# An encoder layer on one core: a block of the second product moved past a product, a half-width root, later stores and waits, eight additions moved to GpSimd

## The chip, the core and the metric

The kernel runs on one core of one Trainium2 chip. The metric is device time of one execution in microseconds (us). A core has five engines that run their own queues in order: TensorE (PE in the profile, with its weight loads as PEld), VectorE (DVE), ScalarE (ACT), GpSimd (POOL) and SyncE (SP), which here only starts DMAs. Data lies in SBUF (128 partitions), matrix products land in PSUM, large arrays in DRAM.

## The reference, cut to what matters

One layer of a transformer encoder for two requests, 512 and 1024 tokens, model width 1024, all in float32. The parts that the change touches are the MLP and the gated embedding behind it:

```
m = _rmsnorm(h, norm_mlp_g)
h = h + jnp.square(jax.nn.relu(m @ w_up)) @ w_down            # 1024 -> 4096 -> 1024
gate = jax.nn.sigmoid(_rmsnorm(h, norm_ple_g) @ w_ple_gate)   # 1024 -> 1024
h = h + gate * (p_i @ w_ple_proj)                             # 256 -> 1024
return _rmsnorm(h, final_norm_g)
```

Ahead of it stand a normalisation, an input projection, attention with rotary positions beside a pooling mixer, and an output projection.

## The kernel before, in words

**Precision.** Every float32 operand is split into a high part in a reduced format and a low part, the rest (a cast on ScalarE, then a subtraction on GpSimd or VectorE). A product is three matmuls: high by high, high by low, low by high (`three`, line 103).

**Tiling.** The 1536 tokens are three chunks of 512, numbered 0 (the short request), 1 and 2. Activations lie transposed, features on partitions. SBUF is 49 equal buffers (`slot`, line 74); a tile takes a free one, and a program orders who waits for whose release.

**The MLP.** Matrix products are done by a scheme with seven products of halves in place of eight (numbered 1 to 7, taken in the order 1, 6, 2, 5, 7, 3, 4), whose sums and differences are made on VectorE. `Pair(c, g)` (line 987) is the up product for 256 of the 4096 hidden features; there are 16 pairs for chunk 0 (`c` = 0) and 16 for chunks 1 and 2 together (`c` = 1, called wide here).
- For chunk 0, `Pair.run` (line 1082) makes the seven products with 256 columns a matmul, in PSUM tiles `px` (products 1 and 2), `py` (6), `pz` (5 and 3) and `pq` (7 and 4), takes Relu and Square, and splits the result into `r` (lines 1119, 1125 high; 1129 low, on VectorE). The down product of a pair is made while the next pair's products run: `between(i)` (line 1629) calls the pair before's `down(i)` for one of four blocks of 12 matmuls of 512 columns each (PSUM tile `pd`), which VectorE adds to `h` (line 1080). In the kernel before, block 0 stands between products 1 and 6, block 1 between 2 and 5, block 2 between 7 and 3, block 3 behind 4.
- For the wide pairs, `Pair.run_wide` (line 1132) makes seven products of 12 matmuls of 512 columns. ScalarE copies product 1 (line 1137) before product 2 may be added to the same PSUM tile. The results are four quarters, `c1` and `c2` with two halves each; `c2`'s second half is ready after product 7, its first half after product 4. Relu and Square of `c2` run over both halves behind product 4 (lines 1162, 1163). `inputs` (line 1166) splits quarters and differences into tiles `ta` (cast in 1172, low part in 1174, differences in 1177) and stores them to DRAM as `T_d`. The down product of the wide pairs comes afterwards (`Double`, line 1181): it loads `T_d` as `tb`, splits weights `v` (casts in 1206), makes blocks `pd`, and evacuates them (1241, 1243) into `H` and `U`, a term shared by parts 2 and 3 of chunk 1's rows and by all four parts of chunk 2's (a part is 256 features).

**Side work.** TensorE's order is written out by hand. After each product, `after(i)` (line 1637) issues one step of what feeds later products: `feed` splits the up weights (cast in line 1009, low part on GpSimd in line 1010, sums on VectorE), `split_down` the down weights, `inputs` and `weights` those above, and then calls `step` (line 603). A step first carries out whatever `later(n, ...)` put off by `n` steps (a first-in-first-out list), then moves each generator in `besides` on by one yield, then the first one in `chores`. So a `wait(n)` in a generator is a wait of `n` steps.

**Loads and stores.** `sy.dma_start` starts a DMA from SP's queue where the scheduler sees fit. `load` (line 55) does the same, and ties the DMA behind the last TensorE instruction written so far.

**The gate.** After the down product, `gate` (line 1699) makes eight output blocks of 128 features for chunk 0, eight for chunk 1, then eight for each half (256 tokens) of chunk 2: 6 matmuls for the projection (`pj`), 24 for the gate (`pg`), then a chain VectorE (1733), ScalarE (1734), VectorE (1735, 1736), ScalarE (1737), and GpSimd, which sums squares (1743). Steps are called behind `pj` and at the places that `HOOKS` (line 1694) names: nine a block for chunk 0, nine for chunk 1 (one in its last block), two a block for chunk 2's first half, three for its second. `gate_in` (1508) makes the next chunk's gate input `hg` (1518 on ScalarE, 1520 on VectorE) in the last block. `split_pp` (1502) splits the embedding in block 6 (1505, 1506).
- `stat(c)` (line 874) finishes chunk `c`'s rows: `lower` adds `U` (line 881) and scales (882) on VectorE, `total` squares on ScalarE and sums on GpSimd (891); 25 steps later `spread_g` makes the reciprocal root and spreads it over the partitions by matmuls (`ssg`, `bcg`). Chunk 1's runs during chunk 0's gate, chunk 2's during chunk 1's.
- `finish(c, o, w, sq)` (line 1745) runs in `chores` behind each group: it waits some steps, sums the squares by matmuls (`ssf`), makes the root, spreads it (`dgf` in line 655, `bcf`), scales (1769) and stores the result.

**The start.** Nine matmuls on a constant tile (`warm`) run before the first data arrives.

Of the kernel before, what the change touches and what calls it, by code (L numbers as in the profile page):

```python
# [12 lines left out]
ALU = mybir.AluOpType  # L13
# [22 lines left out]
def encoder_layer(ctx, tc, xT, xn, xr, pT, w1, w2, w_pool, w_out, w_up, w_down, w_gate, w_proj,  # L36
# [141 lines left out]
    wz = slot([P, CH], mybir.dt.bfloat16, "warm")  # L178
    gp.memset(wz, 1.0)
    wps = tp_ps("warm")  # L180
    for i in range(9):
        pe.matmul(wps, wz[:, 0:P], wz, start=True, stop=True)
    ones_sb = const.tile([P, P], F32R, name="ones_sb")
    gp.memset(as32(ones_sb), 1.0)
# [410 lines left out]
    def later(n, act, *a):  # L595
        aged.append((age[0] + n, act, a))
# [277 lines left out]
    def stat(c):  # L874
        acc = slot([P, 2, CH], F32, f"sqg{c}")

        def lower(a):
            for e in range(2):
                t = hT[c][a][:, e]
                if c == 2 or a > 1:  # L880
                    ve.tensor_tensor(t, t, U[a % 2][:, e], op=ALU.add)
                ve.tensor_tensor(t, t, ws[c], op=ALU.mult)
                yield

        def total(a):
            sq = slot([P, 2, CH], F32, f"sqg{c}{a}") if a else acc
            sc.activation(sq, hT[c][a], AF.Square)
            yield
            for e in range(2):
                if a:  # L890
                    gp.tensor_tensor(acc[:, e], acc[:, e], sq[:, e], op=ALU.add)
                    yield

        yield from staged(range(4), lower, total)
        gp.tensor_tensor(acc[:, 0], acc[:, 0], acc[:, 1], op=ALU.add)
        yield from wait(25)
        yield from spread_g(c, acc)

    def spread_g(c, acc):
        bc = yield from rsqrt_rows([acc[:, 0]], CH, f"g{c}")  # L900
        t = slot([P, CH], F32, f"bcs{c}")
        sc.copy(t, bc)
        if c:
            bcs[c] = t
            yield
            return

        def keep():
            sy.dma_start(bc_d, t)
            made.add("bc")  # L910
        later(2, keep)

    MO, ws, made = {}, {}, set()
    HF = CH // 2
# [72 lines left out]
    class Pair:  # L987
# [94 lines left out]
        def run(self, between, after):  # L1082
# [12 lines left out]
            self.product(1, x)  # L1095
            sc.copy(t, x)
            after(1)
            between(0)
            y = bank("u", "py")
            self.product(6, y)  # L1100
            ve.tensor_tensor(u2, y, t, op=ALU.add)
            after(6)
            self.product(2, x, False)
            sc.activation(c1[:, A], x, AF.Relu)
            after(2)
# [26 lines left out]
        def run_wide(self, after):  # L1132

            c1, c2 = self.X = [slot([P, 2, CH], F32, f"c{self.id}{i}") for i in range(2)]
            x = tp_ps(f"px{self.id}")
            self.product(1, x)
            sc.copy(c1[:, 1], x)  # L1137
            after(1)
            y = ps("u", f"py{self.id}")
            self.product(6, y)  # L1140
            ve.tensor_tensor(c2[:, 0], y, c1[:, 1], op=ALU.add)
            after(6)
            self.product(2, x, False)
            sc.activation(c1[:, 0], x, AF.Relu)
            sc.activation(c1[:, 0], c1[:, 0], AF.Square)
            after(2)
            z = tp_ps(f"pz{self.id}")
            self.product(5, z)
            ve.tensor_tensor(c2[:, 1], z, c2[:, 0], op=ALU.add)
            after(5)  # L1150
            q = ps("u", f"pq{self.id}")
            self.product(7, q)
            ve.tensor_tensor(c2[:, 1], q, c2[:, 1], op=ALU.add)
            after(7)
            self.product(3, z, False)
            ve.tensor_tensor(c1[:, 1], z, c2[:, 0], op=ALU.add)
            sc.activation(c1[:, 1], c1[:, 1], AF.Relu)
            sc.activation(c1[:, 1], c1[:, 1], AF.Square)
            after(3)
            self.product(4, q, False)  # L1160
            ve.tensor_tensor(c2[:, 0], q, c2[:, 0], op=ALU.add)
            sc.activation(c2, c2, AF.Relu)
            sc.activation(c2, c2, AF.Square)
            after(4)

        def inputs(self):
# [3 lines left out]
            for i, x in ((1, b11), (5, b11), (2, b21), (3, b22), (7, b12), (6, b11), (4, b21)):  # L1170
                t = slot([P, 2, CH], F32R, f"ta{self.id}_{i}")
                sc.copy(t[:, 0], x)  # L1172
                yield
                ve.tensor_tensor(t[:, 1], x, as32(t[:, 0]), op=ALU.subtract)  # L1174
                if i in diffs:
                    out, y, z = diffs[i]
                    ve.tensor_tensor(out, y, z, op=ALU.subtract)  # L1177
                later(3, load, T_d[self.g, i], flat(t))
                yield

    class Double:
# [387 lines left out]
    def gating(c):  # L1569
# [14 lines left out]

        def keep(a):
            for i in range(2):
                sy.dma_start(hg_d[a][i], flat(gin[c, a][i]))
            return iter(())

        while "bc" not in made:  # L1590
# [154 lines left out]
    def finish(c, o, w, sq):  # L1745
        tok = slice(o, o + w)
        if not o:
            yield from wait((14, 4, 3)[c])
        bc = yield from rsqrt_rows(sq, w, f"f{c}{o}")
        if o:  # L1750
            bc, b2 = bc
# [34 lines left out]

    while not fed:
        step()
    groups = ((0, 0, CH), (1, 0, CH), (2, 0, CH // 2), (2, CH // 2, CH // 2))
    for c, o, w in groups:  # L1790
        sq = []
# [2 lines left out]
        for d in range(KD):  # L1794
            if c == 0 and d % 2 == 0 and d:
                load_h(0, d // 2, hl_d[d // 2])
            if d == 4 and c < 2:
                load_pp(c + 1)
            if c < 2 and d == KD - 2:
# [86 lines left out]
```

## Time and profile before

| what | value |
|---|---|
| median of 3 runs | 1734.44 us (1734.39 to 1734.63) |
| the profiled execution | 1735.07 us |
| its span, first to last instruction | 1733.3 us |
| matmuls in the trace | 9028 |
| mean granted TensorE clock | 0.998 |
| ScalarE, GpSimd, VectorE busy | 869.1, 1052.5, 1279.5 us |

The profile is one execution, read by the hardware. A row of the order of time gives the start in us from the span's first instruction, the duration, the engine, the line, the operation, output and inputs, and in brackets how long the engine was idle ahead of it and who ended that. Several instructions of a kind are drawn together, with their count. The ends of matmuls are modelled, so that the last one of a row seems to reach into the next row; what one takes is read from start to start. A line can be that of a helper: line 49 is every matmul, line 56 every `load`.

### The profile page before, as it was taken

To read this page: it belongs to the slowest core of one execution; us is meant where nothing else is said; L and a number is where in the kernel's file an instruction comes from. 1 tells how busy PE (TensorE), PEld (TensorE's weight loads), DVE (VectorE), ACT (ScalarE), POOL (GpSimd) and SP (SyncE) were. 2 spreads that over 40 slices of the span, in tenths; PEclk is the share of its full clock that TensorE was granted. 3 is DMA by queue.
4 is the path that set the end of the run, shared out by engine and by line. 5 is a ranking of instruction groups with operands and counts; after the bars stand their busy time and mean duration, and the time that the engine had idled before them with its cause. 6 is when DMAs were issued, how large, how long until landed. Compare 5 with 4: busy or idle time off the path is not lost.

```text
span 1733.3 us, 25333 instructions
## 1 busy us (share of the span) xinstructions
PE 1704.3 (98%) x9028; PEld 1437.7 (83%) x9028; DVE 1279.5 (74%) x1683; ACT 869.1 (50%) x1515; POOL 1052.5 (61%) x844
## 2 busy tenths in 40 slices
PE   9999999999999999999999999999999999999998
PEld 7888878888889988888887787877787877887788
DVE  6676765788887568767757999998676677665865
ACT  6444355667884575565544666666522113224243
POOL 2485983434666678878855455555678765645432
PEclk9999999999999999999999999999999999999999
DMA  7364645120429525643596766667999595941102
GB/s 259 134 217 162 253 176 201 37 98 14 147 110 355 197 91 165 207 143 132 175 380 246 251 251 233 231 242 265 384 393 368 230 349 213 401 168 61 56 18 86
DMA packets 111150, 351.01 MB, mean 203 GB/s; under 512 B 12465, under 2 KB 18993, under 8 KB 111025
## 3 DMA queue, kind: packets, MB, share of 16 engines
q1 hardware_dynamic: 110464, 349.01, 55.0%
q8 instruction: 71, 1.16, 0.3%
q14 instruction: 55, 0.44, 0.1%
q10 hardware_dynamic: 560, 0.40, 0.1%
HBM read 227.20 MB, written 122.16 MB: 202 GB/s over the span
## 4 chain that ended last, share of the span: by engine, by line
PE 38%; DVE 7%; ACT 3%; issue 1%; POOL 1%; DMA 0%; POOLq 0%; ACTq 0%; DVEq 0%
PE pd L49 18%; PE px L49 5%; PE pz L49 4%; PE pq L49 4%; PE pg L49 3%; PE py L49 2%; PE pj L49 1%; DVE ta L1174 1%; DVE hg L1520 1%; DVE s L1735 1%; DVE H L1736 1%; ACT s L1734 1%; DVE c L1177 1%; DVE h L1769 0%; ACT ta L1172 0%
## 5 line engine op out<-in xcount | busy, mean ns | idle before, releaser
L49 PE MATMUL pd<-tb,v 128*128 128x512 f32 x1344 | 315.5, 396 | 3.8 <-ACT Hu L1241 2.0
L49 PEld LDWEIGHTS pd<-tb,v 128*128 128x128 f32 x1344 | 253.2, 189 | 65.4 <-ACT Hu L1241 2.4
L1010 POOL TENSOR_TENSOR w<-ws,w 128x512 fp32r<-128x512 f32 x128 | 185.0, 1450 | 155.5 <-ACT w L1009 155.5
L49 PE MATMUL pd<-r,wd 128*128 128x512 f32 x768 | 191.3, 396 | 6.2 <-DVE r L1129 5.8
L1010 POOL TENSOR_TENSOR w<-wur,w 128x512 fp32r<-128x512 f32 x96 | 154.3, 1620 | 65.9 <-ACT w L1009 62.0
L49 PE MATMUL z<-w,x 128*128 128x512 f32 (+1 forms) x864 | 174.9, 360 | 0.6 <-DVE x L124 0.6
L536 POOL TENSOR_SCALAR pr<-pr,rr 128x1024 f32<-128x1024 f32 (+1 forms) x96 | 94.8, 988 | 126.6 <-DVE rr L534 61.1
L49 PEld LDWEIGHTS pd<-r,wd 128*128 128x128 f32 x768 | 139.5, 188 | 38.1 <-DVE r L1129 9.4
L49 PEld LDWEIGHTS z<-w,x 128*128 128x128 f32 x864 | 144.2, 190 | 26.7 <-issue 1.5
L1212 POOL TENSOR_TENSOR v<-we,v 128x512 fp32r<-128x512 f32 x80 | 117.9, 1498 | 69.8 <-ACT v L1206 49.7
L1174 DVE TENSOR_TENSOR ta<-c,ta 128x512 fp32r<-128x512 f32 x112 | 126.6, 1130 | 30.8 <-ACT ta L1172 30.7
L49 PE MATMUL pg<-hg,wg 128*128 128x512 f32 (+1 forms) x768 | 142.3, 339 | 1.0 <-DVE hg L1520 1.0
L1243 DVE TENSOR_TENSOR H<-pd,H 128x1024 f32<-128x1024 f32 x72 | 87.8, 1222 | 71.1 <-PE pd L49 71.1
L546 ACT CAST pt<-tp 128x512 fp32r<-128x512 f32 x160 | 88.0, 590 | 101.3 <-PE tp L53 100.4
L547 DVE TENSOR_TENSOR pt<-tp,pt 128x512 fp32r<-128x512 f32 x160 | 104.1, 684 | 41.0 <-ACT pt L546 40.8
L49 PEld LDWEIGHTS pg<-hg,wg 128*128 128x128 f32 x768 | 119.2, 188 | 18.1 <-DVE hg L1520 1.6
L1206 ACT CAST v<-we 128x1024 fp32r<-128x1024 f32 x40 | 41.5, 1049 | 164.5 <-DMA we<-in_w_down_dram 73.5
L1172 ACT CAST ta<-c 128x512 fp32r<-128x512 f32 x112 | 69.3, 620 | 107.8 <-DVE c L1177 107.0
L520 DVE TENSOR_REDUCE nm<-S 128x1 f32<-128x1024 f32 (+1 forms) x96 | 100.2, 1044 | 26.6 <-PE S L49 26.1
L530 ACT ACTIVATE pr<-S,nm 128x1024 f32<-128x1024 f32 (+1 forms) x96 | 94.2, 981 | 12.4 <-DMA qs_d<-qs 6.3
L49 PE MATMUL px<-mw,w 128*128 128x512 f32 x384 | 95.3, 397 | 1.6 <-ACT c L1137 1.4
L49 PE MATMUL o<-pt,vs 128*128 128x512 f32 x320 | 93.2, 403 | 0.8 <-DVE pt L547 0.8
(279 smaller groups left out, 3738.0 us busy)
## 6 DMA issues: line engine op xcount, KB each, us to landing
T_d<-ta SPq DMA_DIRECT2D x112, 512.0 KB, 3.0
tb<-T_d SPq DMA_DIRECT2D x112, 512.0 KB, 9.2
wur<-in_w_up_dram SPq DMA_DIRECT2D x64, 512.0 KB, 5.2
wdr<-in_w_down_dram SPq DMA_DIRECT2D x32, 512.0 KB, 4.4
we<-in_w_down_dram SPq DMA_DIRECT2D x32, 512.0 KB, 8.8
mw_d<-mm SPq DMA_DIRECT2D x28, 512.0 KB, 6.2
mw<-mw_d SPq DMA_DIRECT2D x28, 512.0 KB, 10.1
h_d<-h SPq DMA_DIRECT2D x16, 512.0 KB, 3.0
```

The costliest lines, as they stand in the source:

```text
L49: last_pe[0] = nc.tensor.matmul(*a, **k).ins
L520: ve.tensor_reduce(nm, S[:, :nch * CH], axis=AX.X, op=ALU.max, negate=True)
L530: sc.activation(self.pr[j], S[:, :n], AF.Exp, bias=nm, accum_out=self.sums[:, j:j + 1])
L536: gp.tensor_scalar(p, p, rr, 1.0, op0=ALU.mult, op1=ALU.mult)
L546: sc.copy(self.pt[kt][:, 0], tp)
L547: ve.tensor_tensor(self.pt[kt][:, 1], tp, as32(self.pt[kt][:, 0]), op=ALU.subtract)
L1010: gp.tensor_tensor(t[:, 1], x, as32(t[:, 0]), op=ALU.subtract)
L1172: sc.copy(t[:, 0], x)
L1174: ve.tensor_tensor(t[:, 1], x, as32(t[:, 0]), op=ALU.subtract)
L1206: sc.copy(hi, src)
L1212: gp.tensor_tensor(lo[:, p], src[:, p], as32(hi[:, p]), op=ALU.subtract)
L1243: ve.tensor_tensor(H[at], pd, H[at], op=ALU.add)
```

## The change

Nine edits:
1. Ten `warm` matmuls in place of nine.
2. In `stat`, chunk 2's rows are no longer added to `U` on VectorE (chunk 1's still are, for the two of four parts that need it there).
3. A new generator `complete(2)` makes these eight additions on GpSimd, one every `EVERY` = 2 steps, put into `besides` at block `FROM` = 5 of chunk 0's gate, parts in the order 0, 2, 1, 3.
4. In `Pair.run`, `between(0)` moves from behind `after(1)` to behind `after(6)`: block 0 of the pair before's down product comes after product 6.
5. In `run_wide`, Relu and Square of `c2` are split: its second half behind product 7, its first half behind product 4.
6. `T_d` stores are put off by 4 steps in place of 3.
7. The store of the spread root `bc_d` is put off by 4 in place of 2 steps, and is a `load`.
8. The stores of `hg_d` are put off by 4 steps and are `load`s.
9. `finish` waits 14, 6, 4 steps for chunks 0, 1, 2 in place of 14, 4, 3.

```diff
-    for i in range(9):
+    for i in range(10):
         pe.matmul(wps, wz[:, 0:P], wz, start=True, stop=True)
...
         def lower(a):
             for e in range(2):
                 t = hT[c][a][:, e]
-                if c == 2 or a > 1:
+                if c == 1 and a > 1:
                     ve.tensor_tensor(t, t, U[a % 2][:, e], op=ALU.add)
                 ve.tensor_tensor(t, t, ws[c], op=ALU.mult)
                 yield
...
+    def complete(c):
+        for a in (0, 2, 1, 3):
+            for e in range(2):
+                t = hT[c][a][:, e]
+                gp.tensor_tensor(t, t, U[a % 2][:, e], op=ALU.add)
+                yield from wait(EVERY)
...
         def keep():
-            sy.dma_start(bc_d, t)
+            load(bc_d, t)
             made.add("bc")
-        later(2, keep)
+        later(4, keep)
...
             self.product(1, x)
             sc.copy(t, x)
             after(1)
-            between(0)
             y = bank("u", "py")
             self.product(6, y)
             ve.tensor_tensor(u2, y, t, op=ALU.add)
             after(6)
+            between(0)
             self.product(2, x, False)
...
             self.product(7, q)
             ve.tensor_tensor(c2[:, 1], q, c2[:, 1], op=ALU.add)
+            sc.activation(c2[:, 1], c2[:, 1], AF.Relu)
+            sc.activation(c2[:, 1], c2[:, 1], AF.Square)
             after(7)
...
             self.product(4, q, False)
             ve.tensor_tensor(c2[:, 0], q, c2[:, 0], op=ALU.add)
-            sc.activation(c2, c2, AF.Relu)
-            sc.activation(c2, c2, AF.Square)
+            sc.activation(c2[:, 0], c2[:, 0], AF.Relu)
+            sc.activation(c2[:, 0], c2[:, 0], AF.Square)
             after(4)
...
-                later(3, load, T_d[self.g, i], flat(t))
+                later(4, load, T_d[self.g, i], flat(t))
...
         def keep(a):
             for i in range(2):
-                sy.dma_start(hg_d[a][i], flat(gin[c, a][i]))
+                later(4, load, hg_d[a][i], flat(gin[c, a][i]))
             return iter(())
...
         if not o:
-            yield from wait((14, 4, 3)[c])
+            yield from wait((14, 6, 4)[c])
...
+    EVERY, FROM = 2, 5
     groups = ((0, 0, CH), (1, 0, CH), (2, 0, CH // 2), (2, CH // 2, CH // 2))
...
+            if c == 0 and d == FROM:
+                besides.append(complete(2))
```

## The prediction

> **What bounds the kernel now.** I read the page's engine totals first, then TensorE's waits, then the order of time around each wait. In a row of waits stand the engine and tile that waited, who ended the wait, and us in total, times, longest.
>
> ```profile
> span 1733.3 us, 25333 instructions
> PE 1704.3 (98%) x9028; PEld 1437.7 (83%) x9028; DVE 1279.5 (74%) x1683; ACT 869.1 (50%) x1515; POOL 1052.5 (61%) x844
> ```
>
> ```profile
> PE pd L49 <- DVE r L1129: 5.8, 7, 1.5
> PE ssf L49 <- POOL s L1743: 3.0, 2, 1.7
> PE pd L49 <- ACT Hu L1241: 2.0, 1, 2.0
> PE px L49 <- ACT c L1137: 1.4, 3, 0.9
> ...
> PE bcf L49 <- DVE dgf L655: 1.1, 2, 0.8
> PE pg L49 <- DVE hg L1520: 1.0, 2, 0.7
> ...
> PE pd L49 <- ACT r L1125: 0.4, 2, 0.2
> ```
>
> TensorE works 1704.3 of 1733.3 us. The change removes no matrix work, so what can be won lies in 29 us of idle time and in what ending rows hide of it. Most of the waits listed are met by some edit: `pd` on `r` (second product's first block), `ssf` (`finish`), `px` on `c` (last root), `bcf` (VectorE in chunk 1's gate). `pd` on `Hu` isn't: its queue is looked at below.
>
> **Edit A: the first block of a pair's down product goes behind product 6.** An undisturbed pair and the most delayed kind, in order of time (start, duration, engine):
>
> ```profile
> 590.04 2.95 PE L49 MATMUL pd<-r,wd 128*128 128x512 f32 x12
> 592.82 1.59 PE L49 MATMUL py<-mo,w 128*128 128x256 f32 x12
> ...
> 674.77 1.30 POOL L1010 TENSOR_TENSOR w<-ws,w 128x512 fp32r<-128x512 f32 x1 [4.38 <-ACT w L1009]
> 674.92 0.86 PE L49 MATMUL pd<-r,wd 128*128 128x512 f32 x3
> 676.59 1.26 DVE L1129 TENSOR_TENSOR r<-c,r 128x512 fp32r<-128x512 f32 x1 [1.68 <-ACT c L1126]
> 677.90 2.12 PE L49 MATMUL pd<-r,wd 128*128 128x512 f32 x8 [1.47 <-DVE r L1129]
> 679.86 1.57 PE L49 MATMUL py<-mo,w 128*128 128x256 f32 x12
> ```
>
> Undisturbed, `pd` takes 592.82 - 590.04 = 2.78 us of start to start. In the disturbed pair it takes 679.86 - 674.92 = 4.94, so 2.16 are lost where the rows of idle time show at most 1.63 (1.47, and 0.16 for `r L1125`): modelled ends hide a quarter. The 5.8 + 0.4 = 6.2 us of the wait rows then stand for about 6.2 x 2.16 / 1.63 = 8.2 us. Product 6 is twelve matmuls 256 wide, 1.4 us start to start (half of `pd`'s 2.78; they are half as wide). Put ahead of `pd`, it gives VectorE 1.4 us more to finish the low half of `r`. The longest wait is 2.16, all others are below 1.4, so they go whole; the two longest (the row's 1.5, about as in this pair) would leave 0.7 each.
>
> What is late next is in the same fence: GpSimd's low half of product 6's weights ends at 674.77 + 1.30 = 676.07. Product 6 would start at 674.92 and want it at its third matmul, 0.23 later: a wait of 0.9 us in that pair, which swallows the 0.7. Where `r` is on time the weights are early too, as both hang on the same ScalarE queue. I take 8.2 - 2 x 0.9 = 6.4 us gained. Bounds: 4.3 (6.2 - 1.9, if the rows hide nothing) to 8.2. The evacuation of the block on VectorE (`L1080`) only slides behind `u2`; its bank is wanted again two blocks later.
>
> **Edit B: `finish` waits longer.** TensorE stands in both of these:
>
> ```profile
> 1666.53 1.05 PE L49 MATMUL ssf<-ones_sb,s 128*128 128x1 f32 x8 [1.71 <-POOL s L1743]
> ...
> 1687.30 0.88 PE L49 MATMUL pj<-pp,wpj 128*128 128x256 f32 x6
> ...
> 1690.87 0.86 PE L49 MATMUL pj<-pp,wpj 128*128 128x256 f32 x6
> 1698.01 0.60 PE L49 MATMUL ssf<-ones_sb,s 128*128 128x1 f32 x4 [1.29 <-POOL s L1743]
> ```
>
> An output block of chunk 2's gate takes 1690.87 - 1687.30 = 3.57 us. In its first half there are two steps a block, so two steps more for chunk 1's `finish` move its `ssf` by 3.57 us, against a wait of 1.71. The second `finish` starts when the first has ended, two steps later, and waits one more: three steps, in the half with three a block, again 3.57 us against 1.29. Both waits go: 3.0 us. The results of chunk 1 and of chunk 2's first half, with their stores on SP, then leave up to a block later, still ahead of the last block's chain: no cost at the end. Bounds 2.5 to 3.4.
>
> **Edit C: half of the last root sooner.** The end of one pair of the wide up product, where `px` waits in every pair:
>
> ```profile
> 1143.42 1.06 ACT L1162 ACTIVATE c<-c 128x1024 f32<-128x1024 f32 x1
> 1144.28 2.91 PE L49 MATMUL py<-mw,w 128*128 128x512 f32 x12
> 1144.52 1.06 ACT L1163 ACTIVATE c<-c 128x1024 f32<-128x1024 f32 x1
> 1145.29 0.68 DVE L1177 TENSOR_TENSOR c<-c,c 128x512 f32<-128x512 f32 x1
> 1145.48 0.60 ACT L1009 CAST w<-ws 128x512 fp32r<-128x512 f32 x1
> 1146.06 0.62 ACT L1172 CAST ta<-c 128x512 fp32r<-128x512 f32 x1
> 1146.17 1.29 POOL L1010 TENSOR_TENSOR w<-ws,w 128x512 fp32r<-128x512 f32 x1 [1.96 <-ACT w L1009]
> 1146.58 0.58 ACT L1137 COPY c<-px 128x512 f32<-128x512 f32 x1
> 1147.22 3.02 PE L49 MATMUL px<-mw,w 128*128 128x512 f32 x12
> ```
>
> Product 2 (`px`) starts 1147.22 - 1144.28 = 2.94 after product 6, 0.16 more than the undisturbed 2.78, since it waits for the copy `L1137`. Relu and Square of 1024 columns (1.06 each) become passes of 512 in this place, 0.62 each by `L1172`: ScalarE reaches `L1009` 0.88 us sooner, and pays 2 x 0.62 earlier, between products 7 and 3, with nothing but casts behind. But the cast `L1172` needs VectorE's `L1177`, which ends at 1145.97; it starts at 1146.06 already. So in a regular pair the gain stops there, near nothing. Only the pairs in which ScalarE alone was late (the `px` row: 1.4 us in 3 pairs, longest 0.9) gain: I take 1.0. Bounds 0 and 1.4 + 13 x 0.16 = 3.5 (if the cast comes sooner after all); what it may cost is rival 3. `Hu`'s 2.0 stays: ScalarE is held there by the same cast behind `L1177`.
>
> **Edit D: shared term on GpSimd, in chunk 0's gate.**
>
> ```profile
> 1589.07 1.29 POOL L1743 TENSOR_TENSOR s<-s,s 128x512 f32<-128x512 f32 x1 [5.07 <-ACT s L1737]
> 1591.79 2.41 POOL L1506 TENSOR_TENSOR pp<-pr,pp 128x1024 fp32r<-128x1024 f32 x1 [1.43 <-ACT pp L1505]
> 1594.23 0.69 DVE L1733 TENSOR_TENSOR s<-pg,bcs 128x512 f32<-128x512 f32 x1 [5.90 <-POOL pp L1506]
> 1599.74 5.57 PE L49 MATMUL pg<-hg,wg 128*128 128x512 f32 x23 [0.75 <-DVE hg L1520]
> 1627.18 0.50 PE L49 MATMUL bcf<-dgf,ones_sb 128*128 128x512 f32 x1 [0.82 <-DVE dgf L655]
> ...
> L881 DVE TENSOR_TENSOR H<-H,Hu x12: 683/685/1782, 1544.0 to 1621.6; 128x512 f32<-128x512 f32 x12
> ```
>
> Eight of the twelve `L881` leave VectorE in chunk 1's blocks 0 to 2: 8 x 0.69 = 5.5 us out of a queue whose backlog makes `bcf` wait 1.1. That wait goes. The price is eight GpSimd additions of 1.3 us each (`L1743`, same shape), one every two of nine steps a block, through blocks 5 and 6. Five lie ahead of block 5's `L1743`, ahead of which GpSimd was idle for 5.07: 6.5 us of work into 5.07 of room delay it by about 1.4, and with it the low half of `pp`, whose end releases block 6's `L1733` and so, down the chain, `hg`. `hg` already makes TensorE wait 0.75. Against that, `U`'s two buffers come free a chunk earlier, and the wait of `L1733` for `pp` is one for memory. I take half a microsecond lost there: net 0.6 gained. The root of chunk 1's statistics gets one addition ahead of it on GpSimd, 1.3 us, and TensorE reads it only eight steps on. Bounds: +1.9 (both waits go) to -3.6: the 1.1, less 1.4, less 1.1 for each of three operations of VectorE on that chain that a GpSimd addition shuts out (1782 ns in place of 685, by the last row).
> The Trainium skill, GPSIMD Engine Reference, section Engine selection, advises against this edit: an addition of two SBUF operands belongs on VectorE, about twice as slow on GpSimd. The trace agrees, with 1.29 against 0.69; by that rule the edit costs more than it saves, which would be rival 2's time and not the sum's.
>
> **Edit E: one more matmul to warm up.**
>
> ```profile
> L49 PE MATMUL warm<-warm 128*128 128x512 bf16 x9 | 4.0, 631 | 1.3 <-POOL warm L179 1.3
> ...
> 1.34 4.02 PE L49 MATMUL warm<-warm 128*128 128x512 bf16 x9 [1.34 <-POOL warm L179]
> 5.94 4.77 PE L49 MATMUL z<-w,x 128*128 128x512 f32 x11 [0.58 <-DVE x L124]
> ```
>
> The nine run (4.02 - 0.63) / 8 = 0.42 us apart, so the tenth ends at 5.36 + 0.42 = 5.78, before data arrives: cost nothing, gain nothing. `z`'s first eleven also come (4.77 - 0.63) / 10 = 0.41 apart, against 2.78 / 12 = 0.23 in edit A's fence: if the tenth ended that slow stretch a little after `z` begins, some 8 of them would win 0.2 each, 1.6 us.
> The Trainium skill, TensorE: Matmul & The Clock Gate, Part 1, says that the gate opens after a busy window of about 3.4 us which runs free of the kernel; by that rule closing the gap of 0.58 gains those 1.6 us (rival 1) or nothing, as the window falls; no row here shows where it falls.
>
> **Edit F: stores bound to their turn.** Each is one DMA as before, placed a step later on SP's queue.
>
> ```profile
> SPq L56 <- DVE ta L1174: 234.7, 104, 6.0
> ...
>   POOL v L1212: 15.0, 2
> ```
>
> SP stood 234.7 us in front of `T_d` stores whose data was not there; a step later (a product, 2.8 us) it stands less, and the loads queued behind them come sooner. No TensorE wait names a load, so nothing is gained; the seven `ta` tiles of a pair are held 2.8 us longer. The second row (who waited for `T_d`) says that such a hold has delayed GpSimd before; see rival 4. Stores of `hg` and `bc` lie a whole pair of the down product ahead of their reloads: nothing.
>
> **The sum.** 6.4 + 3.0 + 1.0 + 0.6 = 11.0 us. The profiled execution took 1735.07 (1733.3 of span), the median of the runs is 1734.44; 1735.07 - 11.0 = 1724.1 there, 1723.4 for the median. I say 1723.5.
>
> **Rivals.** 0.2% is 3.5 us, about what a measurement of this kernel can tell from no change.
> 1. The clock opens earlier (edit E): 1723.5 - 1.6 = 1721.9. For: the gap in front of `z` is filled. Against: the slow spacing goes on for 4 us after it. Chance 0.12.
> 2. GpSimd's queue at the border of chunks 0 and 1 fills (edit D at its lower bound, -3.6 for +0.6): 1727.7. For: 1.4 us of overflow and the chain `pp`, `L1733`, `hg`. Against: memory free sooner. Chance 0.15.
> 3. Slower: in each wide pair GpSimd gets ahead of VectorE. For: with `L1009` 0.88 sooner, `L1010` is ready at 1146.17 - 0.88 = 1145.29, just as `L1177` starts (1145.29). Should GpSimd come first, `L1177` is shut out for an addition, 1.8 us in place of 0.68 like the slowest `L881`. The cast, `L1137` and `px` then come 1.1 later in some 14 pairs: 15.4 us, 1738.9. Against: `L1177` follows on VectorE's own queue without a wait, while `L1010` has to be released by ScalarE first. It decides on a few hundredths of a microsecond. Chance 0.10.
> 4. The change doesn't do what it says: with tiles held longer and the side work shifted, waits for memory take the place of the ones removed, half a microsecond in each of the sixteen wide pairs: 1723.5 + 8, and 1.5 at the border: 1733. Chance 0.08.
>
> The forecast keeps 0.55. The range 1719.0 to 1730.5 takes in rivals 1 and 2, edit A at both bounds and edit C at its upper; it leaves out 3 and 4. Faster: 0.55 + 0.12 + 0.15 = 0.82, less 0.01 for the tail beyond rival 2; same: 0.09, rival 4 and that tail; slower: 0.10, rival 3.
>
> **What would show it.** Right: no `pd` wait on `r`, instead two of `py` on `L1010` near 0.9; no `ssf` wait on `L1743`; no `bcf` wait on `dgf`; `px` after `py` still about 3.0 in most wide pairs. Wrong: `L1177` near 1.8 in the wide pairs (rival 3); `hg` waits above 2 us near 1599 (rival 2); `z` at 0.23 apart before 10 us (rival 1); new waits on `ta` or `c` casts (rival 4).

## The result and the profile after

The changed kernel takes 1721.59 us (median of 4 runs, 1719.68 to 1722.79), the kernel before 1734.54 beside it (4 runs, 1734.39 to 1735.75): a ratio of 0.9923, 95% interval 0.9906 to 0.994. Run again later, it came to 1722.26 against 1735.23, 0.9923 again (0.991 to 0.9937). It is faster by 12.95 us by the medians; 11.0 were predicted.

The profiled execution took 1722.18 us. Its page, first lines:

```profile
span 1720.4 us, 25389 instructions
...
PE 1699.2 (99%) x9029; PEld 1439.1 (84%) x9029; DVE 1280.0 (74%) x1675; ACT 875.8 (51%) x1547; POOL 1062.8 (62%) x852
```

TensorE's waits, as before (us in total, times, longest):

```profile
PE py L49 <- POOL w L1017: 2.4, 4, 0.9
PE pg L49 <- DVE hg L1529: 1.9, 2, 1.2
PE px L49 <- ACT c L1144: 1.6, 1, 1.6
PE pd L49 <- ACT Hu L1250: 1.4, 1, 1.4
...
PE py L49 <- ACT w L1016: 0.9, 1, 0.9
```

Lines have moved by 7 to 9 (`L1010` is now `L1017`, `L1137` `L1144`, `L1172` `L1181`, `L1177` `L1186`, `L1241` `L1250`, `L1520` `L1529`, `L1743` `L1752`; the new additions are `L903`). The rows for `pd` on `r`, `ssf` on `s` and `bcf` on `dgf` are gone, and `py` on the split weights is there instead, as forecast. Of the `px` waits one is left, in the third wide pair, and it is longer there than before (1.6, before 0.3). Not forecast: `Hu` fell from 2.0 to 1.4, and `hg` rose from 1.0 to 1.9.

Wait rows don't tell what a wait costs. For that I take the start of the first matmul of each stage from the trace and subtract, in all profiled executions of this study (us). "First 168 `pd`" is from the first to the 169th matmul of the wide pairs' down product; "blocks 4 to 5" is from the start of block 4 of the gate to that of block 5, and so on. "Border" is from the start of block 8 to that of block 9 of the gate, where chunk 0 ends and chunk 1 begins:

| kernel | to pair 0 | chunk 0's pairs (A) | wide pairs (C) | first 168 `pd` (C) | blocks 4 to 5 | 5 to 8 | border (D) | 9 to 12 (D) | 16 to 31 (B, D) |
|---|---|---|---|---|---|---|---|---|---|
| before | 550.61 | 341.63 | 327.97 | 42.74 | 7.83 | 21.24 | 7.95 | 23.84 | 60.40 |
| changed | 548.76 | 336.52 | 324.50 | 40.63 | 7.87 | 21.38 | 13.31 | 22.19 | 55.71 |
| changed, again | 548.86 | 337.98 | 324.46 | 40.62 | 7.87 | 21.38 | 11.91 | 22.19 | 55.71 |
| A alone | 548.53 | 336.48 | 327.93 | 42.72 | 7.85 | 21.25 | 7.92 | 23.82 | 60.40 |
| B alone | 548.90 | 344.25 | 328.02 | 42.74 | 7.83 | 21.24 | 7.93 | 23.83 | 58.06 |
| C alone | 549.79 | 342.93 | 324.53 | 40.42 | 7.83 | 21.28 | 7.86 | 23.83 | 60.30 |
| D alone | 549.27 | 344.36 | 328.03 | 42.70 | 7.83 | 21.24 | 12.47 | 22.14 | 59.18 |
| E alone | 549.09 | 344.23 | 327.91 | 42.70 | 7.83 | 21.24 | 7.96 | 23.82 | 60.36 |
| F alone | 548.70 | 343.00 | 328.15 | 42.54 | 7.83 | 21.34 | 7.85 | 23.84 | 61.68 |
| changed without D | 550.17 | 336.48 | 324.55 | 40.63 | 7.87 | 21.38 | 7.87 | 23.83 | 57.90 |
| D from block 4 | 549.51 | 336.52 | 324.50 | 40.63 | 7.87 | 28.30 | 6.94 | 22.18 | 55.76 |
| D one a step | 548.90 | 338.10 | 324.35 | 40.98 | 7.87 | 22.01 | 9.90 | 22.19 | 55.79 |
| D from block 1 | 549.27 | 338.07 | 324.61 | 40.64 | 10.43 | 21.37 | 6.96 | 22.18 | 55.91 |
| D in two places | 549.33 | 338.03 | 324.52 | 40.62 | 9.72 | 21.41 | 8.16 | 22.22 | 55.81 |

Read down a column, the table shows which edit moves which stage. Most columns repeat to a few hundredths where the edit is the same. Chunk 0's pairs scatter, and the granted clock accounts for it: without A the stage takes 341.6 us in the one execution in which the clock never fell to half there, 342.9 to 343.0 with one such fall, 344.2 to 344.4 with two; with A it takes 336.5 without a fall and 338.0 to 338.1 with one. A fall costs some 1.4 us. Between the profiled executions of before and after, the stages in the table give: start -1.85, chunk 0's pairs -5.11, wide pairs -3.47, first `pd` -2.11, border +5.36, blocks 9 to 12 -1.65, 16 to 31 -4.69. The rest adds 0.6, and the span is 12.9 shorter.

In a wide pair of the changed kernel, in order of time:

```profile
1133.64 0.63 ACT L1171 ACTIVATE c<-c 128x512 f32<-128x512 f32 x1
1134.97 2.91 PE L49 MATMUL py<-mw,w 128*128 128x512 f32 x12
1135.24 0.68 DVE L1186 TENSOR_TENSOR c<-c,c 128x512 f32<-128x512 f32 x1
1135.95 0.62 ACT L1181 CAST ta<-c 128x512 fp32r<-128x512 f32 x1 [0.50 <-DVE c L1186]
1136.47 0.58 ACT L1144 COPY c<-px 128x512 f32<-128x512 f32 x1
1137.73 2.93 PE L49 MATMUL px<-mw,w 128*128 128x512 f32 x12
```

Product 2 follows product 6 after 1137.73 - 1134.97 = 2.76, undisturbed; before it was 2.94. The copy that it needs starts 1.50 behind product 6, where it was 2.30. VectorE's subtraction (`L1186`) ends 0.95 behind it, where it was 1.69: it came sooner as well. Why is told under edit C below.

The border in the changed kernel, in order of time:

```profile
1573.07 5.94 POOL L903 TENSOR_TENSOR H<-H,Hu 128x512 f32<-128x512 f32 x4
1582.71 2.40 POOL L1515 TENSOR_TENSOR pp<-pr,pp 128x1024 fp32r<-128x1024 f32 x1
1585.07 4.67 POOL L903 TENSOR_TENSOR H<-H,Hu 128x512 f32<-128x512 f32 x3
1586.97 8.33 DVE L1529 SCALAR_TENSOR_TENSOR hg<-H,gple_sb,hg 128x512 fp32r<-128x512 f32 x8 [1.31 <-ACT hg L1527]
1588.65 0.97 PE L49 MATMUL pg<-hg,wg 128*128 128x512 f32 x3 [1.17 <-DVE hg L1529]
1590.35 8.09 PE L49 MATMUL pg<-hg,wg 128*128 128x512 f32 x20 [0.73 <-DVE hg L1529]
```

The low half of `pp` starts at 1582.71, behind five additions (the four above and one at 1569.32), and three more stand behind it, beside VectorE's `hg`. Those eight operations take 8.33 us; without edit D they take 5.97 (shown below). TensorE waits for them, and then its matmuls are slow too. The next rows are of stretches of 4 us: their length, the busy time of each engine with its count of instructions (TensorE first), then the granted clock, 1.00 being full speed, and two figures for DMA:

```profile
1589.00:1593.00 4.00, 3.23 (x8) 1.84 (x7) 4.00 (x4) 2.23 (x4) 2.43 (x2) 0.63 0.00 0
1593.00:1597.00 4.00, 4.00 (x11) 3.07 (x10) 3.30 (x6) 0.63 (x1) 0.00 (x0) 0.51 0.00 0
1597.00:1601.00 4.00, 4.00 (x19) 3.26 (x18) 3.97 (x6) 1.70 (x2) 1.56 (x1) 1.00 0.00 0
```

The clock falls to half from 1590.06 to 1596.89: 11 matmuls lie in 4 us in place of 19.

### The profile page after: what moved, and what is told of

Its sections match the earlier page's. It is cut to its first block, busy times and chain, and to the rows that moved or that the text cites. A ratio compares the mean times of both kernels' runs of the same rounds, so it can differ in the third digit from the quotient of the medians.

```text
span 1720.4 us, 25389 instructions
## 1 busy us (share of the span) xinstructions
PE 1699.2 (99%) x9029; PEld 1439.1 (84%) x9029; DVE 1280.0 (74%) x1675; ACT 875.8 (51%) x1547; POOL 1062.8 (62%) x852
## 4 chain that ended last, share of the span: by engine, by line
PE 80%; DVE 4%; issue 3%; ACT 2%; POOL 2%; DMA 0%; POOLq 0%; ACTq 0%; DVEq 0%
PE pd L49 27%; PE px L49 7%; PE pz L49 7%; PE pq L49 6%; PE pg L49 6%; PE o L49 4%; PE S L49 4%; PE tp L53 4%; PE py L49 4%; PE pp L49 3%; PE po L49 3%; PE z L49 3%; PE pj L49 1%; POOL w L1017 1%; DVE c L1186 0%
## 5 line engine op out<-in xcount | busy, mean ns | idle before, releaser
L1017 POOL TENSOR_TENSOR w<-ws,w 128x512 fp32r<-128x512 f32 x128 | 192.3, 1508 | 111.2 <-ACT w L1016 103.7
L1017 POOL TENSOR_TENSOR w<-wur,w 128x512 fp32r<-128x512 f32 x96 | 146.6, 1534 | 101.5 <-ACT w L1016 92.6
L1183 DVE TENSOR_TENSOR ta<-c,ta 128x512 fp32r<-128x512 f32 x112 | 109.1, 974 | 26.3 <-ACT ta L1181 26.2
L1181 ACT CAST ta<-c 128x512 fp32r<-128x512 f32 x112 | 69.4, 620 | 65.3 <-DVE c L1186 64.0
```

What stands on the lines that cost most here:

```text
L1017: gp.tensor_tensor(t[:, 1], x, as32(t[:, 0]), op=ALU.subtract)
```

## The experiments

Eleven other kernels were run, each beside the kernel before on the same chip; ratios are against that.

**A alone.**

```diff
             after(1)
-            between(0)
             y = bank("u", "py")
...
             after(6)
+            between(0)
```

> Edit A alone on the kernel before: block 0 of a pair's down product behind product 6; nothing else. My theory (edit A is the first term of the sum, and what the kernel gained in chunk 0's pairs is all A's): no wait of pd on r; three or four waits of py on GpSimd's w near 0.9 in their place; the stretch from the first to the sixteenth pair 5.1 us shorter than before, nothing moves anywhere else: 1734.5 - 5.1 = 1729.4, between 1728 and 1731. Rival: the pairs of chunk 0 gained by something else that shifts the side work (the stores, the earlier start); then A alone gives what its wait rows show and no more, 4.3 less the new waits of 3.8, about 0.5: 1734.

1727.79 against 1735.88, ratio 0.9955 (0.9943 to 0.9968). Chunk 0's pairs took 336.48, 5.15 less than in the profile of before, and the later stages of the table lie within 0.1 us of it. The first theory holds for the stage. The time lies below its range, at 8.1 us less than before: the profile of before is the one without a fall of the clock in this stage, and the five other profiled executions without A have one or two, 1.4 us each. Its waits, where `pd` on `r` no longer stands:

```profile
PE py L49 <- POOL w L1010: 2.8, 5, 0.8
...
PE py L49 <- ACT w L1009: 0.9, 1, 0.9
```

**C alone.**

```diff
             ve.tensor_tensor(c2[:, 1], q, c2[:, 1], op=ALU.add)
+            sc.activation(c2[:, 1], c2[:, 1], AF.Relu)
+            sc.activation(c2[:, 1], c2[:, 1], AF.Square)
             after(7)
...
-            sc.activation(c2, c2, AF.Relu)
-            sc.activation(c2, c2, AF.Square)
+            sc.activation(c2[:, 0], c2[:, 0], AF.Relu)
+            sc.activation(c2[:, 0], c2[:, 0], AF.Square)
```

> Edit C alone on the kernel before: Relu and Square of the last quarter of a wide pair split, one half behind product 7. Theory 1 (the split is what won 3.5 us in the wide pairs and 2.1 us at the start of the second product of chunks 1 and 2, where I had put 1.0 and 0): the stretch of the wide pairs 3 to 3.5 us shorter, the wait of pd on Hu 1.5 or less, all in all 1734.5 - 5.5 = 1729, between 1728 and 1730. Theory 2 (as my prediction said: the cast stays bound by the subtraction on VectorE, so the regular pairs gain next to nothing; the rest came from the later stores, which let SP go on to the loads): 0 to 1 us in the wide pairs, the wait of pd on Hu stays at 2.0: 1733.5 to 1734.5.

1730.52 against 1735.88, ratio 0.997 (0.9959 to 0.9981). The wide pairs took 3.44 us less, the first `pd` blocks 2.32 less: theory 1, and with F alone leaving both stages as they were, theory 2 has fallen. About two thirds of the second gain are clock: the wait itself is 0.8 shorter. The first two rows are the kernel before around its wait for `Hu`, the other two C alone:

```profile
1224.00:1228.00 4.00, 2.01 (x10) 1.30 (x8) 3.31 (x3) 3.81 (x6) 3.47 (x3) 1.00 0.95 286
1228.00:1232.00 4.00, 4.00 (x11) 3.16 (x12) 4.00 (x3) 2.26 (x3) 4.00 (x3) 0.60 1.02 411
```

```profile
1220.30:1224.30 4.00, 2.82 (x13) 1.97 (x12) 3.31 (x3) 3.00 (x5) 3.48 (x3) 1.00 1.02 407
1224.30:1228.30 4.00, 4.00 (x18) 3.25 (x19) 4.00 (x3) 3.23 (x4) 4.00 (x3) 1.00 1.03 419
```

After the wait of 2.0 the mean clock was 0.60 and 11 matmuls lie in 4 us; after one of 1.2 it stayed at 1.00 with 18. The seven matmuls missing are 7 x 0.23 = 1.6 us at full pace.

**D alone, and the changed kernel without D.** The edit of the first (the other undoes the same lines in the changed kernel):

```diff
-                if c == 2 or a > 1:
+                if c == 1 and a > 1:
...
+    def complete(c):
+        for a in (0, 2, 1, 3):
+            for e in range(2):
+                t = hT[c][a][:, e]
+                gp.tensor_tensor(t, t, U[a % 2][:, e], op=ALU.add)
+                yield from wait(EVERY)
...
+            if c == 0 and d == FROM:
+                besides.append(complete(2))
```

> Edit D alone on the kernel before: chunk 2's eight additions of U on GpSimd, one every two steps from block 5 of chunk 0's gate. Theory 1 (the last additions slow VectorE's subtractions for hg at the border of chunks 0 and 1, and TensorE waits, and its clock falls): from block 8 to block 9 of the gate 5 us longer than before, waits of pg on hg of 1.5 or more, bcf's wait gone, from block 9 to block 12 1.7 us shorter: 1734.5 + 3.5 = 1738, between 1736 and 1739. Theory 2 (the loss at the border is that of the later stores of hg or of the shifted steps): block 8 to 9 as before within 0.5 us, bcf's wait gone: 1734.5 - 1.7 = 1733.

> The changed kernel without edit D: the eight additions stay on VectorE in chunk 1's gate. Theory 1 (edit D costs 5 us at the border and gives 1.7 back at bcf): block 8 to 9 as in the kernel before, the wait of pg on hg below 1, bcf's wait of 1.1 back; 1721.6 - 3.5 = 1718, between 1717 and 1720. Theory 2 (another edit makes the loss at the border): block 8 to 9 as in the changed kernel, and 1721.6 + 1.7 = 1723.3.

D alone: 1736.49 against 1735.88, ratio 1.0002 (0.9993 to 1.0012). Without D: 1722.32 against 1735.88, ratio 0.992 (0.9907 to 0.9934), not to be told from the changed kernel's 0.9923. The mechanism of theory 1 is shown: the border loses 4.5 us with D alone and nothing without it. The waits of D alone, then VectorE's `hg` in the kernel without D:

```profile
PE pg L49 <- DVE hg L1527: 2.4, 3, 1.2
```

```profile
1587.18 5.97 DVE L1522 SCALAR_TENSOR_TENSOR hg<-H,gple_sb,hg 128x512 fp32r<-128x512 f32 x8 [1.31 <-ACT hg L1520]
```

But the price that I had put on it, 3.5 us, was too high in both expectations: D gives back more than the 1.7 of blocks 9 to 12. Without it, blocks 16 to 31 take 57.90 in place of 55.71, since `bcf` then waits three times:

```profile
PE bcf L49 <- DVE dgf L655: 1.8, 3, 0.8
```

From the start of block 4 to that of block 31, (blocks 12 to 16, 28.7 us in every kernel, included) the kernel without D takes 147.60 us, the changed one 149.15 and, when run again, 147.75: D costs between 0.1 and 1.6 us, which the timed runs can't show.

**E alone.** `range(10)` for `range(9)` in the kernel before.

> Edit E alone on the kernel before: ten warm matmuls in place of nine. Theory 1 (the point at which the clock opens does not depend on the number of warm matmuls, and the first data's arrival scatters: edit A alone, with nine, also had z fast from its first matmul at 5.28 us, and the changed kernel without edit D, with ten, had it start at 6.11): no difference, 1735.9 plus or minus 1.5, the slow stretch somewhere between none and ten matmuls. Theory 2 (rival 1 of the prediction: filling the gap before z opens the clock early): z at 0.23 apart from its first matmul and the first qp 1.6 us sooner, 1734.3.

1735.96 against 1735.72, ratio 1.0 (0.9991 to 1.0009): theory 1. What settles it is the start of two other kernels. The first row is A alone, with nine warm matmuls, the second the changed kernel without D, with ten:

```profile
5.28 6.96 PE L49 MATMUL z<-w,x 128*128 128x512 f32 x29
```

```profile
6.11 6.13 PE L49 MATMUL z<-w,x 128*128 128x512 f32 x23 [0.66 <-DVE x L124]
```

In both, `z` has no slow stretch: from its third matmul on it runs 0.23 apart, but for one short wait, where the kernel before had nine at about 0.43. So the clock was open with nine and with ten, and `z` came at 5.28 in one and 6.11 in the other. Over the table, pair 0 starts at 549.3 us on average with nine (six executions) and at 549.2 with ten (eight). The profiled execution of the kernel before happened to have the latest start of all, 550.61: in it the granted clock rose to full at 10.28 us, in the thirteen others between 4.27 and 6.76.

**F alone.** `later(4, ...)` for the three kinds of stores, as in the change.

> Edit F alone on the kernel before: the stores of T_d one step later, those of the spread root and of hg four steps later and tied to their turn. Theory 1 (as the prediction said, no wait of TensorE names a load or a store's tile): no difference, within 1 us at every stage, 1735.9 plus or minus 1.5. Theory 2 (the tiles held longer cost waits for memory, in the wide pairs or at the border of chunks 0 and 1, and are part of the 5 us lost there): block 8 to block 9 of the gate 1 us longer or more, or new waits in the wide pairs: 1737 or more.

1736.16 against 1735.72, ratio 1.0001 (0.9992 to 1.001): theory 1, but for one stage that lies outside its 1 us. Blocks 16 to 31 take 61.68 in place of 60.40, since in this execution the clock fell to half for 6.8 us behind the `ssf` wait of 1.7, which the kernel before has as well; A and C alone, without F, show such a fall there too (3.4 us). SP stands less in front of the `ta` stores (234.7 us before), and nothing comes of it:

```profile
SPq L56 <- DVE ta L1174: 153.4, 72, 5.1
```

**B alone.** `(14, 6, 4)` for `(14, 4, 3)`.

> Edit B alone on the kernel before: finish waits 14, 6, 4 steps in place of 14, 4, 3. Theory 1 (edit B of the prediction): both waits of ssf on GpSimd's sum of squares, 1.7 and 1.3, are gone, the stretch from block 16 to block 28 of the gate 3.3 us shorter, nothing elsewhere: 1735.8 - 3.0 = 1732.8, between 1731.5 and 1734. Theory 2 (the waits were an overlap of late rows, and chunk 2's blocks wait for something else next, as for the spread root, whose wait of 0.8 showed in the last half when the additions stayed on VectorE): one of the two goes, 1734.5.

1733.95 against 1735.23, ratio 0.9987 (0.9978 to 0.9995). Blocks 16 to 31 are 2.3 us shorter, between the two theories: neither `ssf` wait on `s` is left, but a third wait of `bcf` has come (2 of them, 1.1 in all, before):

```profile
PE bcf L49 <- DVE dgf L655: 1.7, 3, 0.8
```

VectorE is late there by the eight additions that edit D takes away. B alone gains 2.3, D alone 1.2 in these blocks, both together 4.7. D alone has a fall of the clock there, behind the `ssf` wait of 1.3 that is left, so how the 4.7 divide is not settled. No kernel with B has such a fall in these blocks; four of the six without it do.

**D placed elsewhere.** Four variants of the changed kernel: `FROM = 4`; `EVERY = 1`; `FROM = 1` with `EVERY = 4`; and the eight additions split in two places:

```diff
-            if c == 0 and d == FROM:
-                besides.append(complete(2))
+            if c == 0 and d in (1, 5):
+                besides.append(complete(2, (0, 2), 1) if d == 1 else complete(2, (1, 3), 2))
```

> The changed kernel with FROM = 4 in place of 5: the same eight GpSimd additions, one every two steps, but one output block sooner, so that the last of them is done before the low half of pp and before VectorE makes hg for chunk 1. Theory 1 (the 5.4 us lost at the border come from the last three additions, which slow VectorE's subtractions for hg, and from the clock that falls after TensorE's wait): block 8 to block 9 at 7.9 as in the kernel before, VectorE's eight hg operations in 6.0 us in place of 8.3, bcf's wait gone as well; 1722 - 4 = 1718, between 1716 and 1720. Theory 2 (eight additions are too much for GpSimd anywhere in these blocks): the wait moves to an earlier block, and the time stays at 1722.

1724.54 against 1735.72, ratio 0.9942 (0.993 to 0.9955). The border is healed, 6.94 us, and yet the time is no shorter: blocks 5 to 8 lost 6.9. Theory 1 was right on the border and forgot the root of chunk 1's statistics; the wait moved to an earlier block, as theory 2 had it. Its power (`L638`) stands on GpSimd behind the additions, TensorE waits for it, and the clock falls afterwards (9 matmuls of `pg` in 3.38):

```profile
1573.90 1.73 POOL L903 TENSOR_TENSOR H<-H,Hu 128x512 f32<-128x512 f32 x1
1576.83 1.26 POOL L903 TENSOR_TENSOR H<-H,Hu 128x512 f32<-128x512 f32 x1
1578.05 1.01 POOL L638 TENSOR_TENSOR rsg<-rsg,mhalf 128x4 f32<-128x4 f32 x1
...
1580.14 0.51 PE L49 MATMUL bcg<-dgg,ones_sb 128*128 128x512 f32 x1 [3.71 <-DVE dgg L655]
1582.56 3.38 PE L49 MATMUL pg<-hg,wg 128*128 128x512 f32 x9
```

> The changed kernel with EVERY = 1: the eight GpSimd additions are written one a step from block 5, and queue up in a row ahead of that block's sum of squares and of the low half of pp. Theory 1 (what hurts is an addition beside VectorE's hg operations): all eight are over before hg, whose eight operations take 6.0 us; but pp's low half comes 3 us or more later than in the kernel before, so block 6's chain is late and hg still waits for VectorE, by 1 us or so; the border costs less than 5.4, and the time is 1719 to 1721. Theory 2 (what hurts is the late pp, not the additions beside hg): the border costs 5 us or more as in the changed kernel, 1722 or more.

1720.31 against 1735.72, ratio 0.9916 (0.9903 to 0.993). `hg` takes 5.90, and the border 9.90 in place of 11.9 to 13.3, although `pp` starts 13.9 us behind the start of block 6 (1586.52 - 1572.67), where it was 12.1 in the changed kernel (1582.71 - 1570.58): theory 1. What the late `pp` costs shows as waits of 0.9:

```profile
PE pj L49 <- POOL pp L1515: 0.9, 1, 0.9
PE pg L49 <- DVE hg L1529: 0.9, 1, 0.9
```

> The changed kernel with FROM = 1 and EVERY = 4: the eight GpSimd additions spread thinly over blocks 1 to 4 of chunk 0's gate, ahead of the root of chunk 1's statistics and of hg. Theory 1 (an addition costs only where its neighbour on GpSimd or VectorE is awaited by TensorE: the root's chain with FROM = 4, hg with FROM = 5; in blocks 1 to 4 nothing is): no wait of bcg, no wait of hg beyond the 0.7 of the kernel before, bcf's wait gone, block 8 to block 9 at 7.9 or less: 1722 - 4.5 = 1717.5, between 1716 and 1719.5. Theory 2 (the squares of chunk 1's rows, summed by GpSimd in the same blocks, come late by the additions, and the root with them): a wait of bcg of 1 us or more, and 1720 or more.

1720.41 against 1735.23, ratio 0.9912 (0.9899 to 0.9926). The border takes 6.96, but blocks 4 to 5 lost 2.6, and to neither theory's wait: the split of the gate's weights `wg` stands behind additions and squares on GpSimd.

```profile
PE pg L49 <- POOL wg L1495: 2.1, 2, 1.7
```

> The changed kernel with its eight GpSimd additions in two places: four in a row at the start of block 1 of chunk 0's gate, where GpSimd stands idle for 5 us ahead of the squares that ScalarE has yet to give it, and four from block 5 on, one every two steps, behind the root of chunk 1's statistics and done before the low half of pp. Theory 1 (an addition costs only what stands behind it on GpSimd or beside it on VectorE and is awaited by TensorE): no wait of bcg, of wg, none of hg above 0.7; block 4 to block 5 at 7.8 and block 8 to block 9 at 6.9 to 7.9; against the variant with FROM = 1, which lost 2.6 between blocks 4 and 5, 1720.4 - 2.6 = 1717.8, between 1716 and 1719.5. Theory 2 (the additions in block 1 slow VectorE's work on chunk 1's rows, and the squares, the split weights behind them and the root come late): a wait of wg or bcg of 1 us or more, 1720 or more.

1720.16 against 1734.59, ratio 0.9918 (0.9903 to 0.9933). Theory 2, to 1.9 us in blocks 4 to 5: in block 1 the additions stretch VectorE's rows of chunk 1, the squares come late, and `wg` behind them on GpSimd:

```profile
1538.34 4.25 POOL L903 TENSOR_TENSOR H<-H,Hu 128x512 f32<-128x512 f32 x3
1541.35 1.78 DVE L881 TENSOR_TENSOR H<-H,Hu 128x512 f32<-128x512 f32 x1
1545.16 1.30 POOL L891 TENSOR_TENSOR sqg<-sqg,sqg 128x512 f32<-128x512 f32 x1 [2.57 <-ACT sqg L887]
...
1559.36 2.98 POOL L1495 TENSOR_TENSOR wg<-wgr,wg 128x512 fp32r<-128x512 f32 x2
1561.14 4.67 PE L49 MATMUL pg<-hg,wg 128*128 128x512 f32 x19 [1.59 <-POOL wg L1495]
```

Three of the four places do as well as the changed kernel or 1 to 2 us better by their medians; the intervals overlap, so no place is shown to beat it.

## Why the prediction was right, and where it was wrong

**The total** was 1.9 us short (1723.5 said, 1721.59 measured). That is partly luck: errors in both directions cancelled. Between the two profiles A gave 1.3 less than its term and C 4.6 more; B and D together gave 1.0 in place of 3.6; the start gave 1.9, which no edit brought, and the rest took 0.6.

**Edit A: right in mechanism and size.** `pd` on `r` is gone, `py` on `L1010` is there. In the pair that I worked out, product 6 stops at its third matmul as said:

```profile
671.73 1.28 POOL L1017 TENSOR_TENSOR w<-ws,w 128x512 fp32r<-128x512 f32 x1 [4.38 <-ACT w L1016]
672.06 0.40 PE L49 MATMUL py<-mo,w 128*128 128x256 f32 x2
673.07 1.45 PE L49 MATMUL py<-mo,w 128*128 128x256 f32 x10 [0.61 <-POOL w L1017]
```

From the second `py` at 672.06 + 0.12 to the third at 673.07 lie 0.89, of which 0.12 is pace: 0.8 lost. There were four such places and a wait for the cast, not two places (2.4 and 0.9 us of wait rows), and the two profiled executions differ by 5.1 in place of 6.4. Over all profiled executions the stage takes 343.4 without A (six) and 337.3 with it (eight): 6.1. That this comes near 6.4 is partly luck, as the clock was no term of the sum. The wait that A removes made the clock fall in five of the six, which the profile of before did not show, and in four of the eight with A two `py` waits in a row, of 0.9 and 0.8, did so too. In E alone, where A is missing, the same place with a wait of 1.46:

```profile
676.34 3.31 PE L49 MATMUL pd<-r,wd 128*128 128x512 f32 x8 [1.46 <-DVE r L1129]
```

Eight matmuls in 3.31, where the profile of before has 2.12.

**Edit B: nearly right.** 3.0 said; 2.3 alone, as a `bcf` wait follows that D takes away.

**Edit C: the step that failed.** I took 1.0 for it and nothing for `Hu`; it gave 3.5 and 2.1. The failing step is "in a regular pair the gain stops there": it takes the end of VectorE's `L1177`, 1145.97, as fixed. That the cast hangs on this subtraction was right, since in the changed kernel ScalarE stands idle for 0.50 ahead of the cast, waiting for it. But the subtraction itself ends 0.7 us sooner. Where VectorE gained them, some 6 us earlier while product 3 runs, the next rows show, first before, then after:

```profile
1134.14 5.09 POOL L1010 TENSOR_TENSOR w<-wur,w 128x512 fp32r<-128x512 f32 x3 [2.96 <-ACT w L1009]
1138.00 1.78 DVE L1174 TENSOR_TENSOR ta<-c,ta 128x512 fp32r<-128x512 f32 x1
```

```profile
1124.87 3.46 POOL L1017 TENSOR_TENSOR w<-wur,w 128x512 fp32r<-128x512 f32 x2 [2.95 <-ACT w L1016]
1127.81 0.63 ACT L1161 ACTIVATE c<-c 128x512 f32<-128x512 f32 x1 [1.46 <-DVE c L1160]
1128.80 0.68 DVE L1183 TENSOR_TENSOR ta<-c,ta 128x512 fp32r<-128x512 f32 x1
1129.01 0.61 ACT L1016 CAST w<-wur 128x512 fp32r<-128x512 f32 x1
1129.69 1.56 POOL L1017 TENSOR_TENSOR w<-wur,w 128x512 fp32r<-128x512 f32 x1 [1.36 <-ACT w L1016]
```

Before, GpSimd makes three low parts of weights without a break, and VectorE's low part (`L1174`, now `L1183`) beside the third takes 1.78. Edit C puts a Relu and a Square (`L1161`, `L1162`) ahead of the third cast on ScalarE; GpSimd gets its third low part later, and VectorE's takes 0.68. It is so in 14 of the 16 wide pairs: 1.77 to 1.79 in the six kernels without C, 0.68 in the eight with it. VectorE then works without idle time up to the subtraction, and 0.7 of the 1.1 us arrive there. Both parts were needed, and no run separates them: in the profile of before, ScalarE's `L1009` (1146.08) and VectorE's `L1177` (1145.97) end within 0.1 us of each other ahead of the cast, so that either alone would have gained next to nothing. My rival 3 asked only whether VectorE would be shut out more.

The sign that I had named, `px` after `py` still about 3.0 in most wide pairs, failed: it is 2.75 to 2.97 in all but the third. That my upper bound, 3.5, is the value for the pairs is partly chance: 2.4 lie between products 6 and 2, most of the rest between products 2 and 5, which no `px` row names. For `Hu` the same premise cost 2.1: the cast ahead of the copy waits for VectorE's subtraction before and after; it ends 5.16 us behind the first `pd` before and 4.37 in C alone. The stall fell by 0.8 with it, and the half clock behind it went.

**Edit D: the place right, the size wrong.** I took 0.5 us lost at the border in exchange for 1.1; the border lost 4.0 to 5.4, and blocks 9 to 12 and 16 to 31 gained 1.7 and up to 2.2. The price was rival 2's mechanism (the queue at the border), but my step counted the additions ahead of block 5's sum only; the three behind `pp` fell beside `hg`, eight operations, and the half clock came on top. On the other side I read `bcf`'s 1.1 as the whole gain, where one wait of 0.8 cost 1.7.
The Trainium skill, GPSIMD Engine Reference, section Engine selection, advises against an addition of two operands on GpSimd. The runs bear it out as far as this goes: in five placements no one was faster than the kernel with the additions on VectorE by more than the intervals leave open.

**Edits E and F: nothing, as said.** `z` at 0.23 apart before 10 us, which I had named as the sign of rival 1, did appear, but the sign was poor: with nine matmuls five of six executions show it as well, and all eight with ten.
The Trainium skill, TensorE: Matmul & The Clock Gate, Part 1, says that the clock's window runs free of the kernel, so that the point of opening varies from run to run; these traces agree, with openings between 4.27 and 10.28 us.

**Rivals.** Rival 1: not borne out; E alone changes nothing beyond its interval of 1.6 us, and with nine matmuls the clock was open by 6.8 us in five of six executions. Rival 2: happened at the border, and was paid for by C. Rival 3 (GpSimd ahead of VectorE in wide pairs): not at the place that it names, where `L1186` takes 0.68 in every pair; but in the third pair an earlier `L1186` and the `L1183` ahead of it take 1.78 each beside GpSimd's work, and the `px` wait of 1.6 follows. Rival 4: that wait is the largest new stall outside the border that no edit was meant to bring, and C alone has it too (1.5); for the rest the wide pairs got faster.

What stays open: why the clock falls after some waits of about 1.5 us and not after others. The `px` wait of 1.5 to 1.6 brought it in none of the eight profiled executions with C. The traces hold part of an answer, which no run here was made to test. In each execution all changes of the granted clock lie on a grid of 3.413 us, to a thousandth (in B alone the falls at 676.73, 830.33 and 1229.68 are 45 and 117 steps apart). Of the 26 falls ahead of the last 20 us of the span, 24 follow a step of this grid in which TensorE's rows show 1.6 us idle or more; two such steps were followed by no fall, and two falls follow less (1.03 and 1.34). The `px` wait always had less than 1.4 us in any one step.

## What to carry to other kernels

A price taken at an operand's end is no bound until you have asked what sets that end, and whether the edit moves it: here work added to ScalarE delayed GpSimd, and so let VectorE finish sooner. Price a TensorE wait of 1.5 us or more, or two shorter ones close together, with the half clock that may follow, some 1.4 us. Side work moved to an idle engine is to be placed by what stands behind it on that engine and beside it on the one that it locks out: each of five places here moved the wait to another consumer (`hg`, the root, the split weights), and none was shown to beat leaving the work where it was.

## What the runs showed of the hardware

- Waits of TensorE of about 1.5 to 2 us, or two within some 2.5 us that add up to 1.8, can be followed by half the granted clock for 3.41 us or twice that (at 1228.84 us before, 823.77 in the changed kernel run again, 1590.06 to 1596.89 in the changed kernel), with matmuls 0.42 us apart in place of 0.23. It comes in some executions of a kernel and not in others.
- VectorE's operations on two SBUF operands took 1.78 us in place of 0.68 beside GpSimd's additions and subtractions (the `L881` at 1541.35, the `L1174` at 1138.00), and the eight `hg` operations 8.33 in place of 5.97 beside three additions.
- The first data's arrival scatters: `z` started between 5.26 and 6.11 us in fourteen profiled executions.
